# Half sums of the activations kept in DRAM for the seven-product gates of a hybrid trunk layer, and a rearranged schedule beside the merge

## The chip, the cores and the metric

The kernel runs on one core of a Trainium2 chip. The metric is the device time of one execution in microseconds, lower is better. The engines are PE (TensorE, matmuls; PEld are its weight loads), DVE (VectorE), ACT (ScalarE), POOL (GpSimd), and SP (SyncE), which issues the DMAs. Each engine works through a queue of its own in order.

## The reference

Two layers (`DEPTH = 2`) are applied to 640 tokens: 128 context tokens and 512 latent ones. Cut to what matters:

```python
h = rms_norm(x) * (1 + scale) + shift              # 640 x 1024
z = h @ w_in                                       # 1024 -> 5728, shared out among four mixers
o_a = (group_norm(scan_fwd + scan_bwd) + bonus) * silu(g_a)   # RWKV-7, 8 heads of 64
o_b = attention(q, k, v) * silu(g_b)               # 8 heads, low-rank q and kv
o_c = gelu(u) * mix(layer_norm(gelu(vc))) * silu(g_c)         # gMLP in chunks of 128
o_d = real(fft2(f)) * silu(g_d)
proj  = [o_n @ w_branch[n] for n in range(4)]      # 512 -> 1024 each
gates = sigmoid(h @ w_merge + b_merge)             # 1024 -> 4 x 1024
x = x + gate * (sum_n(proj[n] * gates[n]) @ w_out)
```

The bonus is `sum(r * kt * r_k)` over a head times `v`; the group norm takes mean and variance over the 64 channels of a head.

## The kernel before

Activations stand channels by tokens: 128 channels on the partitions, 640 tokens along a row, worked on in two halves Q0 and Q1 of 320. h is a tile of eight such blocks, in two parts, `h_hi` (rounded to fp32r) and `h_lo` (the rest). Each weight block of 128x512 is loaded (`wr`), cast on ACT (`wh`), and its rest is taken on POOL or DVE (`wl`, the helper `split`, L146 and L147). A product is three matmuls: hi by hi, hi by lo, lo by hi.

A layer runs in stages. (1) Attention: the main generator is `attention`, and `mix` draws steps of a second generator in between: first `proj_rkv` (the projections of the recurrence's inputs, twelve chunks of `shifted`), then `fill`, the projections of the other branches, which go to DRAM (`zdr`). (2) `recurrence`, with `fill` beside it. (3) The merge, branch by branch in the order n = 1, 0, 2, 3, each in four pairs of output blocks. For a pair the gate `h @ w_merge` is computed and then the branch product `o @ w_branch`, which `branch` multiplies and adds into `mg`. Beside each branch another generator makes a later branch's input: `rec_out` (o_a) beside n=1, `gmlp` beside n=0, `fourier` beside n=2, the next layer's modulation beside n=3. `mix` gives `RATE_M` steps of it to each step of the merge. (4) The output projection and the next layer's norm.

A planner (Tile) takes the program in this order and, with times of its own, fixes the order of each engine's queue, the tiles' places and the waits.

A pair's gate is made in one of two ways. The first `PLAIN` pairs of a layer use `dense`: 2 x 2 x 8 x 3 = 96 matmuls. The others use seven products of a 2x2 block scheme in place of eight, `product`, 7 x 4 x 3 = 84 matmuls, which need sums of the weight blocks (made on DVE from `sr` and `wr`) and of blocks of h: with h11, h12 the lower four blocks of h in Q0 and Q1 and h21, h22 the upper four, T1 = h12 - h11, T2 = h22 - T1, T4 = h21 - T2, T3 = h22 - h12. T1, T2 and T4 have tiles of their own in the pool `th`; T3 is put over `h[0:4, Q1]`, which only the dense pairs read.

These sums are made in the merge stage. `sums_of_h` is the first thing in the generator beside n=1, ahead of `rec_out`: for each half of the blocks, additions hi + lo (`hsum`, L1151) and subtractions (L1168, L1172, L1176) on DVE, then a cast on ACT (L1163) and the rest on POOL (L1164). `last_sum_of_h` makes T3 when the first product pair begins (L1185 to L1187).

`rec_out` works on four blocks of 128 channels. Each needs three sums over the heads (`sums`: L1094 and L1095 multiply by the block matrix `blk_r`): of y for the mean, of `ks` for the bonus, of the squares for the variance. Each `sums` casts and splits its operand on ACT and POOL (`ch`, `cl`, one buffer each), yields twice, multiplies both halves and yields. `gmlp` normalises five tiles `vt` on DVE (L961 to L963) and multiplies each by `ws` (L967) one step later.

Of the kernel before, what the change touches and what calls it, by code (L numbers as in the profile page):

```python
# [8 lines left out]
F32 = mybir.dt.float32  # L9
# [3 lines left out]
ALU = mybir.AluOpType  # L13
# [14 lines left out]
RATE_M = (0.75, 0.45, 0.6, 0.45)  # L28
PLAIN = 2
# [29 lines left out]
def trunk(ctx: ExitStack, tc: tile.TileContext, A: dict, O: dict, dbg: dict):  # L59
# [153 lines left out]
    xdr = dr.tile([8, 128, T], F32, name="xdr")  # L213

# [127 lines left out]
    def layer(l, X, h, w13):  # L342
# [87 lines left out]
        def proj_rkv(kp, z13):  # L430
# [16 lines left out]
            rows = seq(low_rank(kp, z, 0), low_rank(kp, z13, 1))  # L447
            for nth, c in enumerate((4, 5, 6, 7, 0, 1, 2, 3, 8, 9, 10, 11)):
                z = kp.tile([128, T], F32, tag="k", name="rkv")

                for i, _ in enumerate(shifted(c, z)):
                    if i % 4 == 1 and nth:
                        next(rows, None)
                    yield
# [9 lines left out]
                yield CHUNK_END  # L464
            turn(3, z)

# [459 lines left out]
        def gmlp():  # L926
            with tc.tile_pool(name=f"cd{l}", bufs=1) as c1, tc.tile_pool(name=f"ce{l}", bufs=2) as c2:
# [149 lines left out]
        def rec_out(y):  # L1077
            with tc.tile_pool(name=f"gn{l}", bufs=2) as gp:
                def load(c):
                    rv = []  # L1080
                    for i, (src, row) in enumerate(((spill, c), (spill, 12 + c), (spill, 4 + c), (thdr, 4 + c), (thdr, 12 + c))):
                        rv.append(gp.tile([128, T], F32, tag=f"rv{i}", name=f"rv{i}", bufs=2 if i > 2 else 1))
                        nc.sync.dma_start(rv[i].rearrange("p (c t) -> p c t", t=128), src[l][:, :, row, :].rearrange("c p t -> p c t"))
                    return rv

                def sums(x, use):

                    hi, lo = (gp.tile([128, T], F32R, tag="c" + n, name="c" + n, bufs=1) for n in "hl")
                    split(hi, lo, x)
                    yield  # L1090
                    yield
                    for q in HALVES:
                        ps = bank1()[:, :320]
                        mm(ps, blk_r, hi[:, q], start=True, stop=False)  # L1094
                        mm(ps, blk_r, lo[:, q], start=False, stop=True)  # L1095
                        use(q, ps)
                    yield

                rv = load(0)
                for c in range(4):  # L1100
# [8 lines left out]
                    V.scalar_tensor_tensor(ks, rv[0], p["rk"][:, c:c + 1], ks, op0=ALU.mult, op1=ALU.mult)  # L1109
                    yield  # L1110
                    yc = tmp()
# [35 lines left out]
        def hsum(kk, top, q):  # L1147

            ks = slice(4 * top + 2 * kk, 4 * top + 2 * kk + 2)
            t = tmp().rearrange("p (k t) -> p k t", k=2)  # L1150
            V.tensor_add(t, h_hi[:, ks, q].bitcast(F32), h_lo[:, ks, q].bitcast(F32))  # L1151
            return t

        def sums_of_h(tp, B):

            for n in ("1", "2", "4"):
                B["T" + n] = tuple(tp.tile([128, 4, 320], F32R, name=f"T{n}{x}") for x in "hl")
            for kk in range(2):
                ks = slice(2 * kk, 2 * kk + 2)

                def put(n, t):
                    hi, lo = (x[:, ks, :] for x in B[n])
                    S_.copy(hi, t)  # L1163
                    G.tensor_sub(lo, t, hi.bitcast(F32))  # L1164

                t1 = hsum(kk, 0, Q0)
                t = hsum(kk, 0, Q1)
                V.tensor_sub(t1, t, t1)  # L1168
                put("T1", t1)
                yield  # L1170
                t2 = hsum(kk, 1, Q1)
                V.tensor_sub(t2, t2, t1)  # L1172
                put("T2", t2)
                yield
                t4 = hsum(kk, 1, Q0)
                V.tensor_sub(t4, t4, t2)  # L1176
                put("T4", t4)
                yield

        def last_sum_of_h(B):  # L1180

            for kk in range(2):
                ks = slice(2 * kk, 2 * kk + 2)
                a, b = hsum(kk, 1, Q1), hsum(kk, 0, Q1)
                V.tensor_sub(a, a, b)  # L1185
                S_.copy(h_hi[:, ks, Q1], a)
                V.tensor_sub(h_lo[:, ks, Q1], a, h_hi[:, ks, Q1].bitcast(F32))  # L1187
            B["T3"] = h_hi[:, 0:4, Q1], h_lo[:, 0:4, Q1]
            B["11"] = h_hi[:, 0:4, Q0], h_lo[:, 0:4, Q0]
            B["21"] = h_hi[:, 4:8, Q0], h_lo[:, 4:8, Q0]  # L1190
            B["22"] = h_hi[:, 4:8, Q1], h_lo[:, 4:8, Q1]
# [484 lines left out]
```

## Time and profile before

| | |
|---|---|
| median of 3 runs | 2366.4 us (2363.68 to 2366.9) |
| the profiled execution | 2370.31 us |
| its span, first to last instruction | 2368.4 us |
| mean granted clock of TensorE | 0.971 of 2.4 GHz |
| PE busy | 2168.4 us, 92% |
| DVE busy | 1681.2 us, 71% |
| ACT busy | 1195.0 us, 50% |
| POOL busy | 911.2 us, 38% |

Times in the rows are microseconds from the span's start unless marked ns. A row of a line names line, engine, operation and the tiles written and read. A wait is idle time of an engine and what ended it. In layer 0 the attention stage runs from about 80 to 395 us, the recurrence from there to 721, the first branch of the merge (n=1) to 846, n=0 to about 955, the rest of the merge to about 1155; layer 1 runs about 1174 us later.

### The profile page before, as it was taken

The numbers are of one execution on the slowest core, as the hardware profiler recorded it, in microseconds if no ns is written. First come the engines' busy times: TensorE is split into PE (matmuls) and PEld (weight loads), VectorE is DVE, ScalarE is ACT, GpSimd is POOL, SyncE is SP. The second block draws the span as 40 slices with busy tenths as digits, with TensorE's granted clock in tenths as the row PEclk, the third lists the DMA queues.
The fourth block names the chain that finished last, engine by engine and source line by source line (L and its number), as shares of the span: only waits on it lengthen the run. The fifth ranks groups of instructions, "written<-read, shape, count | busy, mean of one in ns | idle before, by whom it ended". The sixth has DMA issues, their size and how long they took to land. (4 is left out here: it accounts for less than half of the span.)

```text
span 2368.4 us, 49971 instructions
## 1 busy us (share of the span) xinstructions
PE 2168.4 (92%) x19356; PEld 1979.3 (84%) x19356; DVE 1681.2 (71%) x3182; ACT 1195.0 (50%) x2607; POOL 911.2 (38%) x906
## 2 busy tenths in 40 slices
PE   6899998999997889999998999979999977999998
PEld 3788897788887788997998888978888877989997
DVE  4777758988877876554456787589888679766554
ACT  4566754444434563554445676534444345545542
POOL 2322125444436443342452212254444364342443
PEclk8999999999999899999999999999999998999999
DMA  7233326232225365346532323362332254543332
GB/s 257 60 108 88 106 88 205 78 111 89 77 66 174 96 208 199 114 138 209 173 99 85 102 81 100 113 204 82 94 94 64 59 182 124 190 148 107 105 106 96
DMA packets 210317, 288.98 MB, mean 122 GB/s; under 512 B 27168, under 2 KB 119968, under 8 KB 210080
## 3 DMA queue, kind: packets, MB, share of 16 engines
q1 hardware_dynamic: 210080, 285.79, 38.5%
q8 instruction: 152, 2.49, 0.5%
q14 instruction: 85, 0.70, 0.1%
HBM read 227.37 MB, written 58.36 MB: 121 GB/s over the span
## 5 line engine op out<-in xcount | busy, mean ns | idle before, releaser
L147 POOL TENSOR_TENSOR wl<-wr,wh 128x512 fp32r<-128x512 f32 x315 | 435.0, 1382 | 874.1 <-ACT wh L146 740.1
L170 PE MATMUL dps<-hhi,wh 128*128 128x320 f32 x1472 | 489.8, 333 | 7.2 <-ACT hhi L302 4.2
L172 PE MATMUL dps<-hhi,wl 128*128 128x320 f32 x1472 | 466.3, 317 | 13.5 <-POOL wl L147 13.5
L171 PE MATMUL dps<-hlo,wh 128*128 128x320 f32 x1472 | 468.1, 318 | 9.5 <-DVE hlo L304 4.7
L146 ACT CAST wh<-wr 128x512 fp32r<-128x512 f32 x372 | 229.9, 619 | 255.3 <-PE dps L171 126.4
L170 PEld LDWEIGHTS dps<-hhi,wh 128*128 128x128 f32 x1472 | 283.3, 192 | 16.6 <-ACT hhi L302 5.0
L171 PEld LDWEIGHTS dps<-hlo,wh 128*128 128x128 f32 x1472 | 283.4, 193 | 16.1 <-POOL hlo L304 7.6
L172 PEld LDWEIGHTS dps<-hhi,wl 128*128 128x128 f32 x1472 | 283.1, 192 | 15.3 <-POOL wl L147 15.0
L171 PE MATMUL dps<-olo,wh 128*128 128x320 f32 x512 | 159.7, 312 | 5.6 <-DVE olo L147 5.5
L170 PE MATMUL dps<-ohi,wh 128*128 128x320 f32 x512 | 162.1, 317 | 1.0 <-ACT ohi L146 1.0
L824 DVE TENSOR_TENSOR XZ<-XZ,m 128x512 f16<-128x512 f16 x200 | 129.5, 676 | 41.5 <-PE m L821 41.2
L172 PE MATMUL dps<-ohi,wl 128*128 128x320 f32 x512 | 158.9, 310 | 0.0
L147 POOL TENSOR_TENSOR wl<-sr,wh 128x512 fp32r<-128x512 f32 x56 | 84.6, 1510 | 144.2 <-ACT wh L146 127.8
L771 POOL TENSOR_TENSOR GG<-GG,con 64x256 f32<-64x256 f32 x80 | 61.2, 765 | 167.9 <-DVE GG L766 164.9
L170 PEld LDWEIGHTS dps<-ohi,wh 128*128 128x128 f32 x512 | 96.8, 189 | 9.8 <-issue 4.2
L171 PEld LDWEIGHTS dps<-olo,wh 128*128 128x128 f32 x512 | 96.9, 189 | 7.8 <-DVE olo L147 6.3
L172 PEld LDWEIGHTS dps<-ohi,wl 128*128 128x128 f32 x512 | 96.6, 189 | 0.1
L146 ACT CAST wh<-sr 128x512 fp32r<-128x512 f32 x84 | 52.0, 620 | 87.2 <-PE dps L171 48.7
L814 DVE TENSOR_TENSOR T<-m,con 128x256 f16<-128x256 f32 x200 | 80.6, 414 | 17.6 <-PE m L813 17.1
L1199 PE MATMUL dps<-hhi,wh 128*128 128x320 f32 x224 | 73.6, 329 | 7.0 <-ACT g L1266 6.3
L617 DVE TENSOR_TENSOR pl<-m,ph 128x512 fp32r<-128x512 f32 (+1 forms) x96 | 59.0, 619 | 26.3 <-ACT ph L616 25.1
L1201 PE MATMUL dps<-hhi,wl 128*128 128x320 f32 x224 | 72.0, 321 | 3.0 <-POOL wl L147 2.6
(571 smaller groups left out, 6256.0 us busy)
## 6 DMA issues: line engine op xcount, KB each, us to landing
wr<-in_w_in SPq DMA_DIRECT2D x180, 256.0 KB, 3.0
ar<-in_w_ada SPq DMA_DIRECT2D x48, 512.0 KB, 6.0
wr<-in_w_merge SPq DMA_DIRECT2D x72, 256.0 KB, 3.0
wr<-in_w_branch SPq DMA_DIRECT2D x64, 256.0 KB, 2.7
zdr<-f SPq DMA_DIRECT2D x48, 320.0 KB, 3.5
rk<-spill SPq DMA_DIRECT2D x20, 768.0 KB, 5.9
t<-zdr SPq DMA_DIRECT2D x48, 320.0 KB, 3.8
sr<-in_w_merge SPq DMA_DIRECT2D x56, 256.0 KB, 3.1
```

Of the source, the lines that this page charges most:

```text
L146: S_.copy(hi, src)
L147: (leng or G).tensor_sub(lo, src, hi.bitcast(F32))
L170: mm(ps, hi[:, c], ahi(k)[:, q], start=(k == 0), stop=False)
L171: mm(ps, hi[:, c], alo(k)[:, q], start=False, stop=False)
L172: mm(ps, lo[:, c], ahi(k)[:, q], start=False, stop=(k == K - 1))
L617: V.tensor_sub(pl[:, 0:w], tp[:, 0:w], ph[:, 0:w].bitcast(F32))
L771: G.tensor_sub(GK[HALF[j], j], GK[HALF[j], j], bc(i64[HALF[j]], 4))
L814: V.tensor_mul(T1.rearrange("p u (j k o i) -> p (u j) k o i", j=2, o=2, i=b)[:, :, :, 0, :], ps[:, 0:256].rearrange("p (x k i) -> p x k i" ...
L824: V.tensor_add(new, new, ps.rearrange("p (x n i) -> p x n i", x=2, i=b))
L1199: mm(ps, hi[:, c], b[0][:, k, :], start=first and k == 0, stop=False, skip_group_check=True)
L1201: mm(ps, lo[:, c], b[0][:, k, :], start=False, stop=(k == 3), skip_group_check=True)
```

## The change

The sums of h move. A new generator `sums_of_h` in `proj_rkv` makes T1 to T4 for one block of h at a time, all on POOL, in 32 instructions of 128x320 a layer, and stores them to a DRAM tensor `tdr`. Two of its steps are drawn for each chunk of the projections after the first. In the merge `load_sum` loads a sum into the place of its lo part, casts the hi part on ACT and subtracts on DVE: T1 and T2 after the first gate of the first pair, T3 and T4 when the product pairs begin. `PLAIN` becomes 1, so 15 pairs of 16 in a layer use seven products.

In `rec_out` the operands of the three head sums are split earlier (`two`, two buffers each for `ch` and `cl`), the squares on DVE and the others on POOL, and `pause` puts steps between split and product; the load of `rv4` has one buffer in place of two. In `gmlp` the product by `ws` comes one tile later than the normalisation and there are more steps; `RATE_M` for n=0 goes from 0.45 to 0.5.

```diff
-RATE_M = (0.75, 0.45, 0.6, 0.45)
-PLAIN = 2
+RATE_M = (0.75, 0.5, 0.6, 0.45)
+PLAIN = 1
...
+    tdr = [dr.tile([4, 128, 4, 320], F32, name=f"tdr{l}") for l in range(L)]
...
             rows = seq(low_rank(kp, z, 0), low_rank(kp, z13, 1))
+            sums = sums_of_h()
             for nth, c in enumerate((4, 5, 6, 7, 0, 1, 2, 3, 8, 9, 10, 11)):
...
                 for i, _ in enumerate(shifted(c, z)):
                     if i % 4 == 1 and nth:
                         next(rows, None)
+                    if i % 4 == 3 and nth:
+                        next(sums, None)
                     yield
...
+            run(sums)
             turn(3, z)
...
+        def sums_of_h():
+            Q0, Q1 = HALVES
+            for k in range(4):
+                f1, f2 = tmp(tag="f"), tmp(tag="f")
+                quarters = (f1[:, Q0], k, Q0), (f1[:, Q1], k, Q1), (f2[:, Q1], k + 4, Q1), (f2[:, Q0], k + 4, Q0)
+                t1, t3, t2, t4 = (x[0] for x in quarters)
+                for t, kk, q in quarters:
+                    G.tensor_add(t, h_hi[:, kk, q].bitcast(F32), h_lo[:, kk, q].bitcast(F32))
+                    if q is Q1:
+                        yield
+                G.tensor_sub(t1, t3, t1)
+                G.tensor_sub(t3, t2, t3)
+                yield
+                G.tensor_sub(t2, t2, t1)
+                G.tensor_sub(t4, t4, t2)
+                for i, t in enumerate((t1, t2, t3, t4)):
+                    nc.sync.dma_start(tdr[l][i][:, k, :], t)
+                yield
...
-                for tt in range(5):
-                    V.tensor_scalar(vt[:, tt, :], vt[:, tt, :], st[:, tt, 0:1], rs[:, tt:tt + 1], op0=ALU.subtract, op1=ALU.mult)
-                    V.tensor_mul(vt[:, tt, :], vt[:, tt, :], gg[:, 0, :])
-                    V.tensor_add(vt[:, tt, :], vt[:, tt, :], gg[:, 1, :])
-                    yield
+                for tt in range(6):
+                    if tt < 5:
...
+                        yield
+                        yield
+                    if tt == 0:
+                        continue
+                    tt -= 1
                     ps = bank1()
...
-                        rv.append(gp.tile([128, T], F32, tag=f"rv{i}", name=f"rv{i}", bufs=2 if i > 2 else 1))
+                        rv.append(gp.tile([128, T], F32, tag=f"rv{i}", name=f"rv{i}", bufs=2 if i == 3 else 1))
...
+                def two(x, leng):
+                    hi, lo = (gp.tile([128, T], F32R, tag="c" + n, name="c" + n) for n in "hl")
+                    split(hi, lo, x, leng)
+                    return hi, lo
+
                 def sums(x, use):
 
-                    hi, lo = (gp.tile([128, T], F32R, tag="c" + n, name="c" + n, bufs=1) for n in "hl")
-                    split(hi, lo, x)
-                    yield
-                    yield
                     for q in HALVES:
                         ps = bank1()[:, :320]
-                        mm(ps, blk_r, hi[:, q], start=True, stop=False)
-                        mm(ps, blk_r, lo[:, q], start=False, stop=True)
+                        mm(ps, blk_r, x[0][:, q], start=True, stop=False)
+                        mm(ps, blk_r, x[1][:, q], start=False, stop=True)
                         use(q, ps)
-                    yield
...
+                    y2 = two(y[:, c, :], G)
...
-                    yield
+                    k2 = two(ks, G)
+                    yield from pause(4)
                     yc = tmp()
-                    yield from sums(y[:, c, :],
-                                    lambda q, ps: V.scalar_tensor_tensor(yc[:, q], ps, -1.0 / 64, y[:, c, q], op0=ALU.mult, op1=ALU.add))
-                    yield from sums(ks, lambda q, ps: V.tensor_mul(rv[1][:, q], rv[1][:, q], ps))
+                    sums(y2, lambda q, ps: V.scalar_tensor_tensor(yc[:, q], ps, -1.0 / 64, y[:, c, q], op0=ALU.mult, op1=ALU.add))
+                    yield
                     sq = rv[2]
                     S_.activation(sq, yc, AF.Square)
+                    s2 = two(sq, V)
+                    yield from pause(2)
+                    sums(k2, lambda q, ps: V.tensor_mul(rv[1][:, q], rv[1][:, q], ps))
+                    yield from pause(3)
                     rs = tmp()
-                    yield from sums(sq, lambda q, ps: V.tensor_scalar(sq[:, q], ps, 1.0 / 64, GN_EPS, op0=ALU.mult, op1=ALU.add))
+                    sums(s2, lambda q, ps: V.tensor_scalar(sq[:, q], ps, 1.0 / 64, GN_EPS, op0=ALU.mult, op1=ALU.add))
...
-        def sums_of_h(tp, B):
...
-        def last_sum_of_h(B):
...
+        def load_sum(i, hi, lo):
+
+            for ks in (slice(0, 2), slice(2, 4)):
+                t = lo[:, ks, :].bitcast(F32)
+                nc.sync.dma_start(t, tdr[l][i][:, ks, :])
+                split(hi[:, ks, :], lo[:, ks, :], t, V)
+            return hi, lo
...
                         yield from dense(A["w_merge"][l, m + j, n], 8, H, lambda q, ps: tanh(j, q, ps))
+                        if i == 0 and j == 0:
+                            for x, t in enumerate(("T1", "T2")):
+                                B[t] = load_sum(x, *(tp.tile([128, 4, 320], F32R, name=t + y) for y in "hl"))
...
                 if i == plain:
-                    last_sum_of_h(B)
+
+                    B["T3"] = load_sum(2, h_hi[:, 0:4, Q1], h_lo[:, 0:4, Q1])
+                    B["T4"] = load_sum(3, *(tp.tile([128, 4, 320], F32R, name="T4" + y) for y in "hl"))
...
-        beside = {1: (lambda: seq(sums_of_h(tp, B), rec_out(y)), RATE_M[0]),
+        beside = {1: (lambda: rec_out(y), RATE_M[0]),
```

## Rows read from the trace of the kernel before

**Rows 1.** Page: busy us (share of the span) xinstructions.

```profile
PE 2168.4 (92%) x19356; PEld 1979.3 (84%) x19356; DVE 1681.2 (71%) x3182; ACT 1195.0 (50%) x2607; POOL 911.2 (38%) x906
```

**Rows 2.** Windows: PE, PEld, DVE, ACT, POOL busy (x), clock, DMA share, GB/s.

```profile
80.00:395.00 315.00, 295.64 (x1899) 272.10 (x1897) 226.71 (x446) 198.55 (x440) 81.92 (x95) 0.99 0.37 108
400.00:500.00 100.00, 90.47 (x1381) 78.77 (x1380) 90.46 (x183) 45.95 (x116) 48.72 (x66) 0.98 0.34 109
600.00:700.00 100.00, 96.73 (x1553) 85.03 (x1552) 84.41 (x186) 43.27 (x107) 42.54 (x55) 1.00 0.22 64
```

**Rows 3.** Windows: first branch of the merge, both layers, and two pairs of it.

```profile
721.30:846.40 125.10, 99.50 (x599) 94.45 (x596) 102.42 (x125) 66.49 (x100) 68.20 (x42) 0.90 0.52 158
1895.70:2020.00 124.30, 99.79 (x598) 95.25 (x596) 101.46 (x125) 66.25 (x100) 67.64 (x42) 0.90 0.52 159
721.30:754.50 33.20, 24.59 (x156) 23.93 (x153) 26.72 (x26) 16.55 (x26) 28.78 (x17) 0.90 0.68 202
822.30:846.40 24.10, 21.14 (x138) 19.92 (x137) 20.01 (x25) 18.33 (x28) 10.18 (x7) 1.00 0.65 210
```

**Rows 4.** Waits of PE, 721 to 847: us in total, times, longest.

```profile
PE dps L172 <- POOL wl L147: 5.9, 1, 5.9
PE m L1094 <- DVE rv L1114: 4.3, 2, 3.4
PE m L1094 <- ACT ch L146: 4.2, 3, 2.3
PE m L1095 <- POOL cl L147: 3.8, 4, 1.2
PE dps L171 <- DVE olo L147: 2.7, 1, 2.7
```

**Rows 5.** Timeline of POOL: start us, us, instruction.

```profile
734.64 1.30 POOL L147 TENSOR_TENSOR wl<-wr,wh 128x512 fp32r<-128x512 f32 x1
```

**Rows 6.** Windows of line L1164 alone: us, POOL busy (x), clock, DMA.

```profile
721.00:735.00 14.00, 10.97 (x6) 0.92 0.86 247
```

**Rows 7.** Timeline of DVE.

```profile
790.15 4.49 DVE L1151 TENSOR_TENSOR t<-hhi,hlo 128x640 f32<-128x640 f32 x3
...
797.37 0.47 DVE L1114 TENSOR_TENSOR rv<-rv,m 128x320 f32<-128x320 f32 x1
```

**Rows 8.** Windows around three stalls.

```profile
730.00:745.00 15.00, 9.02 (x49) 8.69 (x48) 13.19 (x9) 5.19 (x10) 14.10 (x9) 0.77 0.61 177
...
790.00:810.00 20.00, 12.54 (x56) 10.97 (x55) 18.02 (x24) 11.68 (x16) 8.90 (x6) 0.74 0.33 97
870.00:880.00 10.00, 6.74 (x40) 6.50 (x39) 9.35 (x17) 4.09 (x7) 2.98 (x2) 0.83 0.30 100
```

**Rows 9.** Lines of DVE, 721 to 847: busy us, mean ns | idle before.

```profile
L1151 DVE TENSOR_TENSOR t<-hhi,hlo 128x640 f32<-128x640 f32 x5 | 8.8, 1796 | 2.0 <-POOL T1l L1164 2.0
...
L1176 DVE TENSOR_TENSOR t<-t 128x640 f32<-128x640 f32 x1 | 2.1, 2086 | 0.0
...
L1187 DVE TENSOR_TENSOR hlo<-t,hhi 128x640 fp32r<-128x640 f32 x2 | 1.6, 818 | 0.0
```

**Rows 10.** Lines of POOL, 721 to 847.

```profile
L147 POOL TENSOR_TENSOR cl<-rv,ch 128x640 fp32r<-128x640 f32 x8 | 13.7, 1708 | 12.5 <-ACT ch L146 12.4
```

**Rows 11.** Two lines, whole span: ns min/median/max, first and last start.

```profile
L1106 DVE TENSOR_SCALAR rv<-rv,der x8: 553/1456/1737, 736.5 to 1948.2; 128x640 f32<-128x640 f32 x8
...
L1151 DVE TENSOR_TENSOR t<-hhi,hlo x24: 808/819/2182, 367.5 to 1969.0; 128x640 f32<-128x640 f32 x24
```

**Rows 12.** Lines of POOL in the attention stage, 80 to 395.

```profile
L147 POOL TENSOR_TENSOR wl<-wr,wh 128x512 fp32r<-128x512 f32 x46 | 64.6, 1407 | 200.1 <-ACT wh L146 178.2 <-PE sps L594 9.8 <-PE m L622 7.6
```

**Rows 13.** Waits of PE in the attention stage, 80 to 395.

```profile
PE dps L172 <- POOL wl L147: 0.3, 1, 0.3
```

**Rows 14.** Timeline before the first `ws` product, DVE and PE.

```profile
876.02 0.68 DVE L963 TENSOR_TENSOR vt<-vt,gg 128x512 f32<-128x512 f32 x1
...
876.80 2.04 PE L967 MATMUL m<-ws,vt 128*128 128x128 f32 x8 [3.26 <-issue]
```

More of the change, by code (lines that the diff above doesn't have):

```diff
@@ L1081, in load, with pause @@
                     for i, (src, row) in enumerate(((spill, c), (spill, 12 + c), (spill, 4 + c), (thdr, 4 + c), (thdr, 12 + c))):
-                        rv.append(gp.tile([128, T], F32, tag=f"rv{i}", name=f"rv{i}", bufs=2 if i > 2 else 1))
+                        rv.append(gp.tile([128, T], F32, tag=f"rv{i}", name=f"rv{i}", bufs=2 if i == 3 else 1))
                         nc.sync.dma_start(rv[i].rearrange("p (c t) -> p c t", t=128), src[l][:, :, row, :].rearrange("c p t -> p c t"))
                     return rv
+                def two(x, leng):
+                    hi, lo = (gp.tile([128, T], F32R, tag="c" + n, name="c" + n) for n in "hl")
+                    split(hi, lo, x, leng)
+                    return hi, lo
                 def sums(x, use):
-                    hi, lo = (gp.tile([128, T], F32R, tag="c" + n, name="c" + n, bufs=1) for n in "hl")
-                    split(hi, lo, x)
-                    yield
-                    yield
                     for q in HALVES:
                         ps = bank1()[:, :320]
-                        mm(ps, blk_r, hi[:, q], start=True, stop=False)
-                        mm(ps, blk_r, lo[:, q], start=False, stop=True)
+                        mm(ps, blk_r, x[0][:, q], start=True, stop=False)
+                        mm(ps, blk_r, x[1][:, q], start=False, stop=True)
                         use(q, ps)
-                    yield
+                def pause(n):
+                    for _ in range(n):
+                        yield
                 rv = load(0)
@@ L1145, in layer @@
         Q0, Q1 = HALVES
[L1147 to L1152, printed above, removed]
-        def sums_of_h(tp, B):
[L1156 to L1169, printed above, removed]
-                yield
[L1171 to L1178, printed above, removed]
-        def last_sum_of_h(B):
[L1182 to L1191, printed above, removed]
+        def load_sum(i, hi, lo):
[4 more added lines that the diff above has]
+            return hi, lo
         def product(ps, raw, b, leng, first=True):
@@ L1203, in product, with merge @@
                     yield
-        def merge(m1, B, mg, order, before, done, plain):
+        def merge(m1, tp, mg, order, before, done, plain):
             o = []
+            B = {}
             def gates(m):
@@ L1246, in merge @@
                 if i == plain:
-                    last_sum_of_h(B)
+                    B["T3"] = load_sum(2, h_hi[:, 0:4, Q1], h_lo[:, 0:4, Q1])
+                    B["T4"] = load_sum(3, *(tp.tile([128, 4, 320], F32R, name="T4" + y) for y in "hl"))
+                    B["11"], B["21"], B["22"] = ((h_hi[:, k, q], h_lo[:, k, q]) for k, q in (
+                        (slice(0, 4), Q0), (slice(4, 8), Q0), (slice(4, 8), Q1)))
                 src = [A["w_merge"][l, m + j, n][:, 512 * k:512 * k + 512] for j in range(2) for k in range(2)]
@@ L1408, in done @@
             split(now["mh"][:, m, :], mlo[m], mg[m], V)
-        mix(merge(m1, B, mg, (1, 0, 2, 3), before, done, PLAIN), aside(), lambda _: now["rate"])
+        mix(merge(m1, tp, mg, (1, 0, 2, 3), before, done, PLAIN), aside(), lambda _: now["rate"])
         run(now["side"])
```

6 lines of the change are left out of this document (4 added, 2 removed).

## The prediction

> **What bounds the kernel now.** The page first [rows 1]: PE is busy 92% of the span, but its end is set by stages with different limits, so I cut the span by stage. In the attention stage PE works 295.6 of 315 us [rows 2]; the only other engine near a limit is DVE with 72%. In the recurrence DVE does 90.5 and 84.4 us of 100 while PE does 90.5 and 96.7 [rows 2]. The first branch of the merge (n=1, with `rec_out` beside it) is another thing: 125.1 us in layer 0 and 124.3 in layer 1, PE busy 99.5 of them at a mean granted clock of 0.90, DVE busy 102.4 [rows 3]. So PE is not the limit there, DVE nearly is, and PE stands still in named places. The list of waits of that stage [rows 4] is what the change is about: one wait of 5.9 us for POOL's `wl`, 4.3 on DVE's L1114, 4.2 on ACT's `ch`, 3.8 on POOL's `cl`, 2.7 on `olo`. The timelines say who was in front. The `wl` of 5.9 us was made at 734.64, behind the six subtractions of L1164 [rows 5], which fill 11.0 of POOL's 14 us from 721 [rows 6]. L1114 came at 797.37, behind the sums of `last_sum_of_h`, which hold DVE from 790.15 with 4.49 us for three [rows 7]. The waits on `ch` and `cl` are `rec_out`'s own: it gives the cast and the subtraction two steps before the product. Each stall also costs clock: 0.77 in the 15 us from 730, 0.74 in the 20 from 790, 0.83 in the 10 from 870 [rows 8]; 0.74 is a mixture of the levels 2.4 and 1.2 GHz. Busy time by the missing share gives 9.0 x 0.23 + 12.5 x 0.26 + 6.7 x 0.17 = 6.5 us a layer.
>
> **Part by part, per layer.**
>
> *Sums out of the merge.* POOL loses L1164's 11.0 us [rows 6]. DVE loses, in this stage, L1151 (five, 8.8 us), L1176 (2.1), L1187 and its like L1185 (two each, 1.6 us each line) [rows 9]: 14.1 us. The other sums were already made before 721, at the border from attention to recurrence, where I count their removal at nothing: bounds 0 and the 0.82 us that one takes alone by five of them. ACT loses eight casts and gains eight in `load_sum`: nothing. In come eight DVE subtractions of 640 columns, 0.82 each [rows 9] = 6.6 us, and eight loads of 320 KB.
>
> *One pair more by seven products.* 96 gate matmuls become 84. The undisturbed pair at clock 1.00 takes 21.14 us for 138 [rows 3], 0.153 each: 12 fewer save 1.8. DVE gets four additions on the weights and three `wl` of 512 columns and three additions of 320; by columns from the 0.82 for 640 that is 7 x 0.66 + 3 x 0.41 = 5.8, and as some will run beside POOL I take 6.3. POOL's number of `wl` in a pair stays six.
>
> *`rec_out`.* One of three subtractions goes from POOL to DVE: four of 1.71 us off POOL [rows 10] and four of 0.82 = 3.3 onto DVE. The cast and the subtraction now stand five to eight steps before the product in place of two. At 0.75 steps to a yield of six matmuls, two steps are 2.7 yields, 16 matmuls, 2.4 us by the 0.153; five are 6.1 us. The POOL subtraction alone lasts 1.7, with the cast of about half that in front and whatever is queued, so two steps were always short and five are mostly enough. `rv4` loses its second buffer, but its last reader L1105 is the first thing in a turn; cost nothing, bounded by one load late, 3 us by the wait on DVE's L1114.
>
> *What the first branch becomes.* DVE: 102.4 - 14.1 + 6.6 + 6.3 + 3.3 = 104.5 us by present durations. But DVE is slowed beside POOL: L1151 takes 0.81 at best, 2.18 at worst, L1106 0.55 and 1.74 [rows 11]. POOL gives up 11.0 + 6.8 = 17.8 of its 68.2 us. With half of POOL's time falling on such DVE work (bounds: none and all; an estimate, from DVE busy 82% of the stage with part of its work reading PSUM) that gives DVE 9 back: 95.6. At the 0.87 of DVE that the recurrence reaches beside a PE of 90 to 97% [rows 2], the stage would be 95.6 / 0.87 = 110 us, 15 less. Check by the waits: 5.9 + 4.3 + 4.2 + 3.8 + 2.7 = 20.9 us of stalls, 5.4 of clock in two stretches and 1.8 of matmuls are 28 on offer. DVE's load lets through about half. Bounds for the gain: 24 (DVE at 0.95, 101 us) and 5 (rival 2).
>
> The Trainium skill ("SBUF — State Buffer", section "Who interferes with whom") says that a DVE instruction with two SBUF inputs contends with a GpSimd instruction that reads SBUF, and that the later of the two blocks until the first is done. The 0.81 and 2.18 of L1151, which has two such inputs, agree. By it POOL's 17.8 us could give DVE up to 17.8 back, and the stage would be 100 us instead of 110.
>
> *`gmlp`.* The first product waited 3.26 us for `vt`, whose last step DVE ended 0.1 us before it [rows 14]; the products now come a step later. On offer 3.3 and 1.1 of clock; DVE is busy 9.35 of 10 us there [rows 8], so a part returns as DVE time. I take 3; bounds 0 and 4.4.
>
> *Attention.* POOL gets 32 instructions of 320 columns. A 512-column one takes 1.41 us there [rows 12], so 0.88 each by columns, 28 us; POOL goes from 82 to 110 of 315. They lie under PE's matmuls. In POOL's queue they stand ahead of `wl` for the projection chunks and the 13 edge copies of the shift; `wl` waited there mostly for its own cast [rows 12], and PE for it once, 0.3 us [rows 13], so there is cover of one or two such instructions. Sixteen stores of 160 KB go through SP's queue ahead of weight loads; DMA share is 0.37. The price is DVE: half of 28 = 14 us more on an engine that is busy 227, so 241 of 315. Bounds 0 and 14; PE follows DVE in this stage only through the softmax chain, so I take 3, near the lower.
>
> *Loads of the sums.* 2.6 MB more in the first two pairs, of them 1.3 MB beside the first, which moves 202 GB/s over 33.2 us [rows 3]; 1.3 MB more makes it 241. T3 also overwrites `h_lo`, so its load on SP waits for the first pair's last gate matmul, and the next weights stand behind it if the planner puts them there. Cost nothing, because 48 branch matmuls (7 us) and six further products lie between; bounds 0 and 5.
>
> **Sum.** -15 - 3 + 3 = -15 a layer, -30 for two. The profiled execution took 2370.3 us (span 2368.4 and 1.9 around it), so 2340; the median of the runs shown is 3.9 lower, so 2336.
>
> **Rivals.**
>
> 1. All the stalls go. The stage comes to 101 us, `gmlp` gives 4.4 and attention costs nothing: 2 x 28.4 = 57, so 2310 against the median. For: every listed wait has a named operand that is now made earlier. Against: DVE, which must then be at 0.95.
> 2. DVE is the bound and takes the gain. It holds 104.5 us of work, gets nothing back from POOL, and 104.5 / 0.87 = 120: 5 less a layer. With 3 and 3 for the others this is -10, so 2356. For: DVE was busy 102.4 of 125.1, and in the stretch from 790 it was 18.0 of 20. Against: there it ran the very sums that go.
> 3. Slower: the attention stage pays. Every us of the 28 that POOL works there stops DVE, and the softmax chain passes it to PE: +28 - 18 = +10 a layer, 2386. It decides from 18 of the 28 on. For: PE has 19 us of slack in 315 and DVE already follows it closely. Against: 88 us of DVE are idle there, and DVE's largest pieces read PSUM. [...]
>
> Less than either: the planner, which orders every engine's queue from its own times, moves something elsewhere. It had moved part of the old sums some 350 us ahead, to 367.5 [rows 11], so it can.
>
> **How the numbers follow.** Forecast (2318 to 2352) 0.56; rival 1 (below 2318) 0.13; rival 2 (2352 to 2368) 0.20; rival 3 0.11. About 0.2%, 4.7 us, is what a measurement tells from no change: half of rival 2 lies within it. Faster 0.56 + 0.13 + 0.09 = 0.78; same 0.11; slower 0.11. The range 2310 to 2364 leaves out under one in ten below and about one in eight above; the forecast's own range is 2318 to 2352.
>
> **What would show it.** Right: the stretch from the last recurrence product to the end of n=1's last pair is 105 to 115 us with a clock above 0.95; the first gate's `wl` wait is gone; PE's waits at the block sums come to under 4 us a layer in place of 12; no wait over 1 us before the first `ws` product; POOL about 28 us more in attention with PE's stretch from the first scores to the last at most 5 us longer. Wrong: PE waiting for `wl` or for softmax pieces in attention; casts of T1 to T4 on ACT with weight casts stuck behind them; DVE above 105 us in the first branch; or a stall of like size at another place of the merge.

## The result and the profile after

The changed kernel takes 2393.1 us (median of 4) against 2366.6: ratio 1.0117, interval 1.0099 to 1.0134. It is slower by 26.5 us; the forecast was 30 faster. The profiled execution took 2392.4 us, its span 2390.7, 22.3 more than before.

The page's first part, as [rows 1]: PE and DVE work as long as before, POOL 39 us longer.

```profile
PE 2168.6 (91%) x19332; PEld 1979.5 (83%) x19332; DVE 1673.5 (70%) x3182; ACT 1197.8 (50%) x2619; POOL 949.8 (40%) x950
```

So time was lost in waits, and the stages show where. The table is made from first and last instructions. The scores are the products into `sps`. The recurrence begins at its first product of `Qs` and `Ks` and ends at the last of `ZZ` and `GG`. A branch ends at its last product with `ohi`. Times are us, layer 0 / layer 1; layer 1 begins at the end of layer 0's merge:

| stretch | before | after |
|---|---|---|
| to the first scores | 124.9 / 136.3 | 139.8 / 150.2 |
| scores | 189.5 / 191.1 | 189.6 / 189.5 |
| border: last scores to recurrence | 80.6 / 80.8 | 74.5 / 73.9 |
| recurrence | 326.4 / 327.6 | 330.1 / 330.2 |
| merge, n=1 | 125.2 / 124.4 | 120.7 / 123.6 |
| merge, n=0 | 107.0 / 96.6 | 110.7 / 100.3 |
| merge, n=2 and n=3 | 206.3 / 180.5 | 205.8 / 180.2 |

Two things went wrong. Ahead of the scores 14 to 15 us a layer are lost, and the merge, which was to pay for all, gives 1 us in layer 0 and costs 3 in layer 1.

**Ahead of the scores.** POOL's timeline in the changed kernel: L480 are the additions of the sums, L483 to L487 their subtractions.

```profile
81.11 4.41 POOL L480 TENSOR_TENSOR f<-hhi,hlo 128x320 f32<-128x320 f32 x4
...
91.41 3.38 POOL L480 TENSOR_TENSOR f<-hhi,hlo 128x320 f32<-128x320 f32 x4 [0.80 <-DMA tdr<-f]
...
99.95 5.43 POOL L480 TENSOR_TENSOR f<-hhi,hlo 128x320 f32<-128x320 f32 x4 [1.02 <-DMA tdr<-f]
...
108.15 0.86 POOL L487 TENSOR_TENSOR f<-f 128x320 f32<-128x320 f32 x1
108.96 2.50 POOL L147 TENSOR_TENSOR wl<-wr,wh 128x512 fp32r<-128x512 f32 x2
```

In layer 0 all but eight of the layer's 32 instructions stand here in one run, from 81 to 109 us, and the `wl` that PE needs next comes behind them at 108.96. The program draws them two steps to a chunk, over some 200 us. In the trace each block of sums begins as soon as the store of an earlier one has freed an `f` buffer (the waits for `tdr`), so the planner put them as early as the two `f` buffers let it. PE's wait there, and windows of the attention stage (which answers to [rows 2]) and around the wait (columns as there):

```profile
PE dps L172 <- POOL wl L147: 11.8, 1, 11.8
```

```profile
80.00:410.00 330.00, 301.21 (x1923) 277.65 (x1922) 227.96 (x444) 201.12 (x445) 104.98 (x125) 0.97 0.38 112
100.00:110.00 10.00, 0.00 (x0) 0.00 (x0) 4.63 (x4) 0.72 (x1) 9.76 (x9) 0.52 0.21 75
110.00:120.00 10.00, 9.68 (x49) 9.09 (x50) 5.83 (x11) 6.21 (x12) 3.01 (x5) 0.80 0.30 91
```

The wait of 11.8 us answers to the 0.3 us of [rows 13]. PE does nothing from 100 to 110, and the clock is granted at 0.52 and then 0.80 of 2.4 GHz, that is, in part at the 1.2 GHz level, after PE stood still. Up to the first scores PE stands still 13.0 us longer than before and works 1.9 us longer: together the 14.9 us.

In layer 1 the loss has the same size but another path. There `wl` costs PE 1.4 us in two waits. The sums hold up POOL's edge copies of the token shift (L365 and L366), ACT stands still for them, and PE waits for a copy that ACT makes later. The lines, from the timelines of POOL, ACT and PE:

```profile
1258.31 2.28 POOL L480 TENSOR_TENSOR f<-hhi,hlo 128x320 f32<-128x320 f32 x2
...
1266.17 0.19 POOL L365 COPY t<-xa 128x2 f32<-128x2 f32 x1
1266.51 0.83 ACT L367 ACTIVATE xa<-xa,der 128x640 f32<-128x640 f32 x1 [9.38 <-POOL t L366]
...
1273.65 0.63 PE L170 MATMUL dps<-hhi,wh 128*128 128x320 f32 x1 [4.62 <-ACT xa L1307]
```

Windows of layer 1 up to the first scores, the kernel before and then the changed one:

```profile
1159.90:1296.20 136.30, 126.92 (x800) 119.14 (x799) 82.46 (x149) 69.06 (x142) 60.85 (x56) 0.99 0.38 118
```

```profile
1171.20:1321.40 150.20, 134.12 (x801) 126.51 (x799) 88.85 (x149) 68.70 (x142) 91.36 (x88) 0.91 0.40 125
```

PE stands still 6.7 us longer, and works 7.2 us longer on the same matmuls at a granted clock of 0.91 for 0.99. That the place in POOL's queue is the cause in both layers is shown by the runs below.

**The first branch.** Both layers, as [rows 3]:

```profile
734.00:854.70 120.70, 95.49 (x586) 90.76 (x585) 99.79 (x137) 68.10 (x107) 54.84 (x32) 0.92 0.60 189
1915.10:2038.70 123.60, 97.72 (x585) 93.01 (x586) 99.53 (x137) 68.42 (x107) 56.30 (x32) 0.89 0.59 185
```

DVE works 99.8 and 99.5 us, not the 95.6 of the prediction, and its share is 0.83 and 0.81, not 0.87. PE's waits there, as [rows 4] (L1125 and L1126 are the block sums, once L1094 and L1095):

```profile
PE m L1125 <- ACT ch L146: 9.5, 3, 4.9
PE m L1126 <- POOL cl L147: 7.2, 3, 5.2
PE aps L1200 <- DVE g L1282: 2.9, 2, 2.7
```

The `wl` wait of 5.9 us is gone, and the one on DVE's L1114. The block sums wait 16.7 us all the same, for 12.3 before. The longest is one for POOL's `cl`. DVE's timeline and POOL's at that place:

```profile
771.37 0.81 DVE L1167 SCALAR_TENSOR_TENSOR t<-t 128x640 f32<-128x640 f32 x1
772.11 0.81 DVE L147 TENSOR_TENSOR hlo<-hlo,hhi 128x640 fp32r<-128x640 f32 x1
772.84 1.54 DVE L147 TENSOR_TENSOR T4l<-T4l,T4h 128x640 fp32r<-128x640 f32 x2
774.31 0.81 DVE L147 TENSOR_TENSOR cl<-rv,ch 128x640 fp32r<-128x640 f32 x1
775.05 0.68 DVE L1266 TENSOR_TENSOR sr<-sr 128x512 f32<-128x512 f32 x1
775.65 0.68 DVE L147 TENSOR_TENSOR wl<-wr,wh 128x512 fp32r<-128x512 f32 x1
776.25 0.68 DVE L1267 TENSOR_TENSOR sr<-wr,sr 128x512 f32<-128x512 f32 x1
```

```profile
772.28 6.04 POOL L147 TENSOR_TENSOR cl<-rv,ch 128x640 fp32r<-128x640 f32 x1 [12.85 <-ACT ch L146]
```

POOL's subtraction of 640 columns, 1.71 us on average in [rows 10], takes 6.04. From 771.37 to 776.93 DVE runs eight instructions with two SBUF inputs back to back, three of them splits of T3 and T4 (`hlo`, `T4l`), and POOL ends 1.4 us after the run. This is called a lock-out below: POOL's subtraction seems to get nothing done until DVE's run is over. In layer 1 PE waits 5.2 us at the same place.

**n=0** became 3.7 us longer in both layers. It takes o_a, which `rec_out` makes beside n=1. PE waits for it now: one wait of 1.8 us in layer 0, and 3.1 and 1.1 in layer 1, for 0.2 and 0.3 before.

```profile
PE dps L170 <- ACT ohi L146: 2.3, 2, 1.8
```

```profile
PE dps L170 <- ACT ohi L146: 3.1, 1, 3.1
PE dps L171 <- POOL olo L147: 1.1, 1, 1.1
```

But these waits don't make the 3.7 us of layer 0. Windows of n=0 there, before and after:

```profile
846.60:953.60 107.00, 98.55 (x638) 90.69 (x638) 72.22 (x118) 46.61 (x88) 36.92 (x26) 0.95 0.55 186
```

```profile
854.70:965.40 110.70, 102.12 (x639) 91.27 (x637) 73.23 (x119) 46.32 (x88) 38.98 (x26) 0.95 0.52 176
```

PE stands still 8.5 us before and 8.6 after, since other waits became shorter. The difference is in PE's busy time, 98.6 and 102.1 us for the same matmuls at the same mean clock, and its cause is open.

### The profile page after: what moved, and what is told of

Same layout as the page of the kernel before. It is cut to its first block, busy times and chain, and to the rows that moved or that the text cites. A ratio compares the mean times of both kernels' runs of the same rounds, so it can differ in the third digit from the quotient of the medians.

```text
span 2390.7 us, 50045 instructions
## 1 busy us (share of the span) xinstructions
PE 2168.6 (91%) x19332; PEld 1979.5 (83%) x19332; DVE 1673.5 (70%) x3182; ACT 1197.8 (50%) x2619; POOL 949.8 (40%) x950
## 5 line engine op out<-in xcount | busy, mean ns | idle before, releaser
L170 PE MATMUL dps<-hhi,wh 128*128 128x320 f32 x1408 | 471.1, 335 | 11.0 <-ACT xa L1307 4.6
L172 PE MATMUL dps<-hhi,wl 128*128 128x320 f32 x1408 | 444.3, 316 | 13.3 <-POOL wl L147 13.3
L171 PE MATMUL dps<-hlo,wh 128*128 128x320 f32 x1408 | 445.7, 317 | 11.6 <-POOL hlo L305 6.8
L170 PEld LDWEIGHTS dps<-hhi,wh 128*128 128x128 f32 x1408 | 270.5, 192 | 20.3 <-ACT xa L1307 4.9
L171 PEld LDWEIGHTS dps<-hlo,wh 128*128 128x128 f32 x1408 | 271.1, 193 | 17.2 <-POOL hlo L305 9.7
L172 PEld LDWEIGHTS dps<-hhi,wl 128*128 128x128 f32 x1408 | 270.4, 192 | 14.6 <-POOL wl L147 14.0
L147 POOL TENSOR_TENSOR wl<-sr,wh 128x512 fp32r<-128x512 f32 x60 | 93.9, 1565 | 149.8 <-ACT wh L146 145.4
L1200 PE MATMUL dps<-hhi,wh 128*128 128x320 f32 x240 | 78.4, 327 | 7.0 <-ACT g L1275 3.9
L1202 PE MATMUL dps<-hhi,wl 128*128 128x320 f32 x240 | 77.4, 322 | 5.3 <-DVE wl L147 3.1
L1202 PE MATMUL aps<-hhi,wl 128*128 128x320 f32 x240 | 75.3, 314 | 4.7 <-DVE wl L147 4.7
```

The costliest lines, as they stand in the source:

```text
L147: (leng or G).tensor_sub(lo, src, hi.bitcast(F32))
L170: mm(ps, hi[:, c], ahi(k)[:, q], start=(k == 0), stop=False)
L171: mm(ps, hi[:, c], alo(k)[:, q], start=False, stop=False)
L172: mm(ps, lo[:, c], ahi(k)[:, q], start=False, stop=(k == K - 1))
L1200: mm(ps, hi[:, c], b[0][:, k, :], start=first and k == 0, stop=False, skip_group_check=True)
L1202: mm(ps, lo[:, c], b[0][:, k, :], start=False, stop=(k == 3), skip_group_check=True)
```

## The experiments

Four theories are tried, two for each loss. For the attention stage, theory A: the loss is the place of the sums in POOL's queue. Its rival B: 28 us of POOL work beside DVE cost that much wherever they stand. For the merge, theory D: DVE's work sets the length of the first branch, and waits only change places. Its rival C: single waits (POOL's queue, short steps) set it. After each time stand its ratio to the kernel before, timed beside it, and the 95% interval.

**The sums alone.** The sums and stores added to the kernel before, the merge untouched:

```diff
+            sums = pool_sums()
...
+                    if i % 4 == 3 and nth:
+                        next(sums, None)
...
```

> The kernel before with the POOL sums and their stores to DRAM added to the attention stage and nothing else; nothing reads the stored sums, and the merge makes its own as before. Theory A: they stand in one run ahead of the first wl again, PE waits about 12 us there in each layer, and the kernel takes 2386 to 2396 us. If the loss of the change lay in the merge: 2370 us or less.

2398.8 us, 1.0132 (1.0114 to 1.0150), 3 us above theory A's range. PE's longest wait ahead of the scores, layer 0 and then layer 1:

```profile
PE dps L172 <- POOL wl L147: 12.0, 1, 12.0
```

```profile
PE dps L170 <- ACT xa L1323: 6.9, 1, 6.9
```

So the paths of the two layers are those of the changed kernel, and the expectation's "in each layer" holds for layer 0 alone. To the first scores it is 141.4 and 149.0 us; scores, border, recurrence and merge are within 2.1 us of before. So the whole loss of the change lies in this part, and the rest of the change takes back about 6 us.

**The sums spread.** Each step queued behind the weight rest traced last:

```diff
+                    with tc.issue_after(cur["rest"]):
+                        G.tensor_add(t, h_hi[:, kk, q].bitcast(F32), h_lo[:, kk, q].bitcast(F32))
```

> The changed kernel with one thing more: each step of the POOL sums is queued on POOL behind the weight rests (wl) of the projection chunk in which it is drawn, so the planner can't put 24 of them in one run ahead of the first chunks' wl. Theory A (the place in POOL's queue costs the time): PE's one wait of 11.8 us for wl in each layer is gone, the first scores start at 125 to 128 us in place of 139.8, and the kernel takes 2362 to 2370 us. Theory B (28 us of POOL work beside DVE costs it, wherever it stands): the wait splits up over the attention stage and the kernel stays above 2382 us.

2382.4 us, 1.0064 (1.0041 to 1.0086): at the lower end of B's range, though A's sign came. The 11.8 us wait is gone and the first scores start at 128.7 and 138.5, but the scores take 199.2 and 197.0 us, 9.7 and 5.9 more. One of the new waits of PE:

```profile
233.19 0.47 PE L652 MATMUL m<-ph,vv 128*128 128x128 f32 x1 [3.74 <-DVE rkv L370]
```

L370 ends the token shift on DVE. It needs the edge copies, which POOL made at 231, behind sums that it had begun at 223.5. Next, with those two copies on DVE:

```diff
-            G.tensor_copy(s[:, 0:T:TC][:, 0:2], z[:, 1:T:TC][:, 0:2])
...
+            V.tensor_copy(s[:, 0:T:TC][:, 0:2], z[:, 1:T:TC][:, 0:2])
...
```

> The spread sums on POOL again, with the shift's two edge copies moved from POOL to DVE. In the spread run PE waited 3.7 us for DVE's line of the shift and 4.2 for vv, and the stretch of the scores took 9.7 and 5.9 us more than before. If DVE stood there behind edge copies that stood on POOL behind sums: those waits go, the scores take 190 to 193 us, and the kernel 2366 to 2372. If DVE is slowed by POOL's reading and writing as such: 2378 or more.

2376.5 us, 1.0045 (1.0031 to 1.0059), between the two forecasts. This wait goes and the start is at 126.4, but the scores stay at 197.3 and 197.2. Windows of the scores, this run and then the kernel before, and the copies in this run's list of DVE's lines:

```profile
126.40:323.70 197.30, 186.41 (x1171) 168.80 (x1171) 150.04 (x331) 129.16 (x310) 58.89 (x59) 0.98 0.36 104
```

```profile
124.90:314.40 189.50, 182.42 (x1169) 165.58 (x1170) 143.06 (x311) 128.73 (x309) 39.75 (x55) 1.00 0.34 96
```

```profile
L367 DVE COPY t<-t 128x2 f32<-128x2 f32 x10 | 3.5, 349 | 0.2
...
L368 DVE COPY t<-t 128x2 f32<-128x2 f32 x10 | 1.6, 158 | 0.0
```

DVE is busy 7.0 us longer, 5.1 of them the copies, and the clock is 0.98 for 1.00. None of PE's waits in this stretch names POOL, so B holds in part: spread on POOL, the sums cost the scores 6 to 8 us a layer. How that gets to PE isn't shown; the next runs show that it is not the amount of DVE work.

**The same sums on DVE**, first as the planner likes, then each step queued behind the shift's last DVE operation:

```diff
-                G.tensor_sub(t1, t3, t1)
...
+                V.tensor_sub(t1, t3, t1)
...
```

> The changed kernel with the 32 instructions of the sums on DVE in place of POOL. Theory A2 (the attention stage loses because POOL's queue holds back wl and the shift's edge copies, not because of the work itself): PE's 11.8 us wait is gone, the time to the first scores is 125 to 130, the scores 190 to 193, and the kernel takes 2356 to 2368 us. Theory B2 (any 14 to 28 us more beside the softmax chain goes to PE): 2380 us or more.

> The changed kernel with the sums on DVE, each step queued behind the shift's last DVE operation of its projection chunk. Same work on DVE as in the run with the sums on DVE, where it stood in front of the attention's first chain; same places as in the spread runs, without POOL. If only the place in a queue costs: first scores at 124 to 127, scores 190 to 193, 2350 to 2360 us. If 14 us more on DVE beside the softmax chain costs as the 28 us on POOL did (7.7 us a layer): 2366 or more.

Unspread 2376.0, 1.0040 (1.0023 to 1.0057), between its two forecasts: 137.8 and 144.5 to the first scores, since the planner puts them among and ahead of the attention's first chain on DVE as well. Spread 2365.4, 1.0005 (0.9992 to 1.0017), again between the forecasts: 126.5 and 137.3, scores 192.6 and 192.6. So ahead of the scores the place costs 7 to 12 us a layer on either engine. Once spread, the work costs the scores 2 to 3 us a layer on DVE, though DVE is then busy 11.7 us longer in layer 0, where it costs 6 to 8 on POOL. For the whole kernel spreading gives 10.6 us on DVE. With the attention all but paid for, the kernel is as fast as before and no faster: the merge gives nothing.

**The merge's parts by themselves**, each in the kernel before:

> The kernel before with the new rec_out alone (earlier splits, pauses, squares split on DVE, two buffers for ch and cl, one for rv4). Theory C (the longer distance from split to product pays, and only the loads of the sums spoil it): 8 to 20 us faster than before, 2346 to 2358. Theory D (the first branch is bound by DVE, so waits only change places): within 5 us of before.

> The kernel before with the new gmlp loop and its rate of 0.5 alone. By the prediction's term 6 us faster (2360); if DVE bounds that stretch too, within 3 us of before.

> The kernel before with one dense pair in place of two and nothing else: the sums are made in the merge as before. By the count of matmuls 3.6 us less for two layers. If DVE bounds the first branch, its ten further instructions a layer cost what the 12 matmuls save or more: 2364 to 2374 us.

`rec_out` 2362.6, 0.9981 (0.9971 to 0.9992); `gmlp` 2364.6, 0.9995 (0.9982 to 1.0008); one dense pair 2363.2, 0.9985 (0.9972 to 0.9998). n=1 is 124.1, 125.4 and 124.8 us long: none shortens it by more than 1.1. For the first two the smaller forecast, that of theory D, came. The one dense pair gives 3.0 us (0.5 to 6.6 by the interval), which fits the count of its matmuls and lies outside the forecast by DVE's load, 2364 to 2374. But n=1, which holds the pair, is only 0.4 us shorter in layer 0, so where the 3 us arise isn't shown.

**DVE work taken out of the first branch.** The first run is the kernel before and leaves out the Newton step of `rec_out`. The second is the run with the DVE sums spread and leaves out the subtraction in `load_sum`:

```diff
-                    newton(rs, sq)
...
-                split(hi[:, ks, :], lo[:, ks, :], t, V)
+                S_.copy(hi[:, ks, :], t)
```

> The kernel before without the Newton step of rec_out (three DVE instructions for each of four blocks, 9.8 us a layer by 0.82 each; the group norm is then less exact). DVE the bound of the first branch: 8 to 12 us less a layer, 2343 to 2351. PE's waits set by the two steps from split to product and by POOL's jam, whatever DVE does: under 4 us a layer, 2359 or more.

> The run with the DVE sums spread, without load_sum's eight DVE subtractions a layer (the lo parts stay unsplit sums, so the gates' values change). DVE the bound of the first branch: 6 to 8 us less a layer there, 2349 to 2354. A single long wait the bound: POOL's cl falls from 6.04 us to about 2 and PE's two waits of 5 us go, 8 to 10 us a layer, 2345 to 2350. Neither: within 4 us of 2365.

Without Newton 2344.9, 0.9909 (0.9887 to 0.9930), n=1 in 112.1 and 112.2 us. Without the rests 2352.9, 0.9944 (0.9926 to 0.9963), n=1 in 112.8 and 112.5 for 122.6 and 120.5. n=1 of layer 0 in these two:

```profile
721.60:833.70 112.10, 95.63 (x597) 92.41 (x598) 88.58 (x112) 65.18 (x101) 67.06 (x42) 0.94 0.57 179
```

```profile
723.30:836.10 112.80, 97.38 (x585) 93.14 (x586) 89.41 (x128) 68.76 (x107) 50.55 (x32) 0.92 0.64 201
```

Without Newton DVE is busy 13.8 us less than in [rows 3], and n=1 is 13.1 shorter. PE's waits for the block sums shrink though no step was put between split and product:

```profile
PE dps L172 <- POOL wl L147: 5.9, 1, 5.9
PE m L1095 <- POOL cl L147: 3.3, 4, 1.3
...
PE m L1094 <- ACT ch L146: 1.5, 2, 0.8
```

They are 3.3 and 1.5 for 3.8 and 4.2, and the one on DVE's L1114 is gone, while the `wl` wait stands. No block sum reads Newton's result, so the waits shrank through DVE's queue, or through tiles that came free sooner. This is the run that speaks for D.

Without the rests DVE is busy 10.4 us less than the 99.8 of the run it is made from, and n=1 is 9.8 shorter. But this run doesn't decide between D and C, because the rival's sign came as well: POOL's long `cl` went, and PE waits 8.7 us for the block sums, for 17.2 (9.9 and 7.3) before this edit:

```profile
PE m L1129 <- ACT ch L146: 6.1, 3, 3.2
PE m L1130 <- POOL cl L147: 2.6, 3, 1.2
```

```profile
L147 POOL TENSOR_TENSOR cl<-rv,ch x8: 1532/1551/1571, 740.6 to 1973.9; 128x640 fp32r<-128x640 f32 x8
```

**DVE work put in.** The additions of the sums are held back to the end of the recurrence, once in the kernel before, and once with the three parts of the merge together (a run that comes below, 2360.1 us):

```diff
-            V.tensor_add(t, h_hi[:, ks, q].bitcast(F32), h_lo[:, ks, q].bitcast(F32))
+            with tc.issue_after(cur["rest"]):
+                V.tensor_add(t, h_hi[:, ks, q].bitcast(F32), h_lo[:, ks, q].bitcast(F32))
...
```

> The kernel before with the additions of the sums queued on DVE behind the last addition to y of the recurrence, so that none is made at the border from attention to recurrence. In the changed kernel the stretch from the last scores to the first recurrence product is 6 to 7 us shorter (74.5 for 80.6), which the prediction counted at nothing. If the five additions and three subtractions on DVE there were the cause: that stretch is 74 to 76 us here too, and the merge takes 6 to 10 us more. If not: 80 to 81.

> The three parts together and the additions held back to the end of the recurrence. If the border gives 6 us a layer and the merge's DVE takes the sums at less than that: 2345 to 2355. If the merge pays them back: as the three parts without it, within 4 us.

2379.5, 1.0058 (1.0043 to 1.0073), and 2377.0, 1.0050 (1.0034 to 1.0067). Windows of the first: the border, the same in the kernel before, and n=1:

```profile
314.20:388.50 74.30, 69.69 (x460) 67.10 (x458) 39.26 (x70) 39.24 (x64) 24.21 (x23) 1.00 0.50 155
```

```profile
314.40:394.90 80.50, 73.76 (x484) 70.65 (x482) 48.65 (x81) 41.54 (x70) 29.75 (x27) 0.98 0.50 155
```

```profile
718.00:851.20 133.20, 102.66 (x597) 97.14 (x598) 114.11 (x137) 66.51 (x101) 70.24 (x42) 0.87 0.49 149
```

The border is 6.3 us shorter, as in the changed kernel, so the early sums had cost that; the recurrence takes 2.9 of it back (329.3 for 326.4). n=1 grows by 8.0 with 11.7 more of DVE. With the three parts n=1 takes 134.0 us for 122.2, and the kernel is 17 us slower than without the holding back, which neither forecast had.

**Single waits.** Four runs move single waits. T3 and T4 are loaded after the fourth product, with the DVE sums unspread; `k2` is split on DVE, with them spread; both together, with them spread; and the old sums are begun later, with their POOL rests queued behind weight rests, with the three parts. Of the first two edits:

```diff
+                if i == plain:
+                    B["T3"] = load_sum(2, h_hi[:, 0:4, Q1], h_lo[:, 0:4, Q1])
...
-                    k2 = two(ks, G)
+                    k2 = two(ks, V)
```

> As the run with the sums on DVE, and T3 and T4 are loaded and split after the fourth product of the first seven-product pair in place of ahead of it. In the changed kernel PE waited 4.9 and 5.2 us there for ch and cl while DVE made eight splits of the sums and POOL's cl took 6.04 us. If that burst makes the wait: both shrink below 2 us and the merge of layer 0 is 6 to 10 us shorter than in the run with the sums on DVE. If the waits come from rec_out itself: no difference beyond 3 us.

> The run with the DVE sums spread, with the second operand of rec_out (k2) split on DVE in place of POOL. If the wait of 5.2 us is POOL kept out by DVE's run of two-input instructions: it goes, 4 to 6 us less a layer, 2354 to 2358. If DVE is the bound: its 3.3 us more a layer turn up elsewhere, 2362 to 2370.

> DVE sums spread, k2 split on DVE, and T3 and T4 loaded after the fourth product. If the late load and k2 cure the same wait: as k2 alone, 2356 to 2362. If they cure different ones: 2350 to 2355.

> The three parts with the sums in the merge (2360), and the sums of h begun six steps later, with their POOL subtractions queued behind the weight rests traced by then, so that the second gate's wl is made ahead of them. If that jam is worth its 5.9 us wait and the clock behind it: 6 to 8 us less a layer, 2344 to 2350. If the later sums then meet rec_out on DVE: 2356 to 2362.

Late loads: 2375.5, 1.0039 (1.0024 to 1.0055), no different from the 2376.0 without. Yet the long `cl` is gone. The line's ns min/median/max in a run with the early loads (DVE sums spread; unspread it is 6037 at most) and in this one:

```profile
L147 POOL TENSOR_TENSOR cl<-rv,ch x8: 1555/1562/6038, 742.0 to 1989.1; 128x640 fp32r<-128x640 f32 x8
```

```profile
L147 POOL TENSOR_TENSOR cl<-rv,ch x8: 1552/1731/2023, 745.6 to 1991.1; 128x640 fp32r<-128x640 f32 x8
```

n=1 is 119.0 for 121.1, and n=0 is 112.2 for 110.7: with the lock-out gone n=1 is 2 us shorter, and n=0 takes most of that back. `k2` on DVE: 2358.8, 0.9973 (0.9959 to 0.9988). n=1 takes 116.7 and 117.0 for 122.6 and 120.5, with DVE *less* busy than the 99.8 before this edit, though it got four instructions more:

```profile
723.30:840.00 116.70, 96.54 (x586) 90.75 (x585) 96.72 (x141) 68.78 (x107) 47.11 (x28) 0.93 0.62 196
```

Both together: 2370.2, 1.0008 (0.9997 to 1.0020), worse than `k2` alone and outside both forecasts; why is open. The later POOL rests: 2376.4, 1.0046 (1.0032 to 1.0060), 16 us slower than the three parts without it, and outside both forecasts. The second gate's wait for `wl` is gone, but PE now waits 5.1 us for the `wl` of the branch product, behind five of the same rests; n=1 takes 124.7 for 122.2 and n=0 114.3 for 105.4. The jam was moved and not removed, so this run doesn't price it. Against C stand the late loads: there a named long wait went, and the kernel's time did not change measurably.

**The parts together**, and with `k2` on DVE:

> The kernel before with the new rec_out, the new gmlp with its rate, and one dense pair, but with the sums made in the merge as before. Alone the three gave -3.9, -1.9 and -3.0 us. If they add up: 2355 to 2360. If they share one limit (DVE): 2360 to 2364.

> The three parts with the sums in the merge, and k2 split on DVE. Here POOL's cl never took over 2.0 us, so if the gain of k2 on DVE was POOL's lock-out alone, 3.3 us more of DVE a layer cost what they weigh: 2362 to 2368. If a split on DVE is better as such: 2352 to 2358.

2360.1, 0.9974 (0.9960 to 0.9989): 5.8 of the 8.8 us, on the border of the two forecasts, and the interval tells neither from the other. With `k2` on DVE 2350.5, 0.9926 (0.9912 to 0.9940), 16.6 us faster than before and the fastest with the whole computation. No long lock-out was there to cure, so the split is better placed on DVE as such. n=1, without and with `k2` on DVE:

```profile
721.30:843.50 122.20, 97.31 (x586) 92.22 (x585) 108.16 (x139) 68.00 (x107) 60.94 (x38) 0.92 0.52 162
```

```profile
722.90:840.80 117.90, 96.32 (x585) 91.78 (x586) 107.07 (x141) 66.24 (x103) 61.76 (x34) 0.91 0.52 159
```

DVE is 1.1 us less busy with 3.3 us more to do, and fills 0.91 of the stretch.

**What D explains and what not.** From the windows, n=1 of layer 0 in us:

| run | length | DVE busy | DVE idle |
|---|---|---|---|
| before | 125.1 | 102.4 | 22.7 |
| without Newton | 112.1 | 88.6 | 23.5 |
| additions held back | 133.2 | 114.1 | 19.1 |
| changed kernel | 120.7 | 99.8 | 20.9 |
| DVE sums spread | 122.6 | 99.8 | 22.8 |
| DVE sums, late loads | 119.0 | 98.9 | 20.1 |
| three parts, sums made in the merge | 122.2 | 108.2 | 14.0 |
| the same with `k2` on DVE | 117.9 | 107.1 | 10.8 |

The first three rows have the same schedule of this branch: DVE's idle time stays at 19 to 24 us, and the branch follows DVE's busy time. The three parts together lower the idle time to 14, so the rearranged schedule does pay; DVE's 5.7 us more of work take most of it. With loaded sums in place of made ones DVE has 8.4 us less to do, but its idle time is back at 20 and more, so the branch gains next to nothing. Why it is back is not shown. The late loads say that the lock-out is a small part of it.

## Why the prediction was wrong

It failed at two steps of about the same size, each some 12 us a layer, and n=0 added 7.

*Attention.* "They lie under PE's matmuls ... so there is cover of one or two such instructions." The cost was put at 3 us a layer and bounded by 14; ahead of the scores it was 14.9 and 13.9. The prediction let the sums stand where the program draws them, and named the planner only as a remainder. In layer 0, 24 of 32 stood in one run in POOL's queue ahead of `wl`; in layer 1 they stood ahead of the edge copies. Rival 3 had the right sign and stage but the wrong mechanism: a place in POOL's queue, not the softmax chain. That its 2386 lies nearest to the 2393 is partly luck. A cost in the stretch of the scores, where rival 3 looked for it, is there at 6 to 8 us a layer once the sums are spread on POOL, but not in the changed kernel (189.6 and 189.5).

*The first branch.* "The stage would be 95.6 / 0.87 = 110 us." It was 120.7 and 123.6, by 99.8 / 0.83 and 99.5 / 0.81. That DVE's queue paces it was right, as the run without Newton shows. Two sizes were off. POOL gave up 13 and 11 us, not 18, and by the prediction's own account DVE got 104.5 - 99.8 = 4.7 back, not 9. And the rate of 0.87 came from another stage, as if a stage's share of DVE were fixed: it was 0.79 to 0.91 over these runs, 0.83 beside the loaded sums, 0.89 and 0.91 with the sums made in the merge. Rival 2's time for the stage, 120, came in layer 0, but not by its sum of 104.5 at 0.87. What holds the share down beside the loaded sums stays open.

*The matmuls*: 3.6 us forecast for two layers, 3.0 measured alone. *`rec_out`*: waits for the block sums did not fall to under 4 us; they rose to 16.7, the longest at the lock-out. *`gmlp`*: alone 1.9 us for two layers, not 6, and not told from nothing (0.9982 to 1.0008); its wait went from 3.26 to 1.19, but n=0 grew by 3.7. *The border*, counted at nothing with 4 us as the bound, gave 6.1 and 6.9, of which the recurrence took back 3.7 and 2.6. *The loads of the sums*: none of PE's listed waits names a load.

Left open: what makes n=0 3.7 us longer, why DVE's idle time is high beside the loaded sums, and why the late loads and `k2` on DVE don't go together.

## What to carry to other kernels

Work moved to an idle engine is not spread because the program draws it in steps. A planner that issues what is ready puts it in a lump ahead of work that is needed sooner, so price the lump, and queue each step behind what it must not delay. Where one engine's queue paces a stage, a single wait removed can come back elsewhere. Then write down that engine's busy and idle time for each version: a change pays only if their sum falls, and work taken off can come back as idle time. And work moved to an idle engine isn't free if it slows the busy one: here a split moved from GpSimd to VectorE made VectorE less busy.

## What was not expected of the hardware

GpSimd and VectorE hold each other up in both directions. The prediction had priced only VectorE's side. A GpSimd subtraction of 128x640 that takes 1.55 us took 6.04, in both layers, beside a run of VectorE instructions with two SBUF inputs; with part of that run moved away it took 2.02 at most. The Trainium skill ("SBUF — State Buffer", section "Who interferes with whom") calls the port pair that the two engines share an exclusive lock, and says that the order of issue decides who blocks. If one VectorE instruction were all that GpSimd had to wait for, the wait would be 0.8 us, an estimate from the 0.81 of the trace and that page's rule. Here the instruction took 4.5 us longer, and ended 1.4 us after the whole run. And four splits of 0.82 us moved from GpSimd to VectorE lowered VectorE's busy time by 3.1 us (99.8 to 96.7) and by 1.1 (108.2 to 107.1).
